# Where the copies behind a background sum of weight quarters are issued, and behind what, in a two-layer hybrid decoder trunk

## The chip, the core and the metric

The kernel runs on one core of a Trainium2 chip. The core has a matrix engine (PE in the profile; its weight loads are listed apart as PEld), a vector engine (DVE), a scalar engine (ACT), a general-purpose engine (POOL) and a sequencer that here only issues transfers (SP). Sixteen DMA engines move the data; SP, ACT and POOL each have a queue from which they issue transfers to them. Each engine works through its own instruction stream in order; semaphores tie the streams together.

The metric is the device time of one execution in microseconds (us), lower being better. Times shown are the median over several runs; a profile is one further execution with a trace.

## The reference

The program takes 512 tokens of width 1024 through two layers and a final norm. All arithmetic is float32.

```python
for l in range(DEPTH):                      # DEPTH = 2
    h = rms_norm(x, norm_mix[l])
    (m_qk, m_v, m_o, m_i, m_f, r_x, r_g, a_q, a_k, a_v, a_qi, a_ki, a_w, gates) = split(h @ w_in[l])
    ...                                     # mLSTM -> y_a;  RG-LRU -> y_b;  selected sparse attention -> y_c
    merged = (g_a * (y_a @ w_branch[l, 0]) + g_b * (y_b @ w_branch[l, 1])
              + g_c * (y_c @ w_branch[l, 2]))
    x = x + merged @ w_out[l]
    h = rms_norm(x, norm_ffn[l])
    ff_g, ff_u = split(h @ ffn_up[l], 2)    # hidden width 3072
    ff_g = causal_dwconv(ff_g, ffn_conv_w[l], ffn_conv_b[l])
    x = x + (gelu(ff_g) * ff_u) @ ffn_down[l]
return rms_norm(x, norm_final)
```

## The kernel before

**Weights and their splits.** All large weights lie in one tensor, `wts`, cut into units of 128 partitions by 1024 values (512 KB). SP loads the units one after the other into two `raw` buffers (`dma_to`, L185). A float32 product is made of three products in the fast type: each unit is split into a high part `wh` (ACT, L216) and a low part `wl` (DVE, L217), and PE multiplies `wl` by the input's high part, `wh` by its low part, and `wh` by its high part (L262, L268 and L306). A usual group of eight input blocks is 24 such matmuls. `unit()` asks for splits up to three or four units ahead of use.

**The order of work.** A scheduler turns the program into one instruction stream per engine. It simulates the program with its own idea of times, and sends each instruction as soon as that simulation finds the engine and the inputs free; instructions traced under `tc.high_priority()` go first among those ready. `tc.issue_after(i)`, here wrapped as `after(i)`, adds one rule: what is traced inside may not stand ahead of `i` on `i`'s own engine. On the chip the streams then run in just that order.

**A layer** begins with the norm of four tiles of 128 tokens (`Norm`: the sum of squares, its power -0.5 as `rs` on POOL, the scaled tile `xn` on DVE, transposes on PE, and a split into `xh`, `xl`). Then come the sections `mv` (four units), `sm` (one group; the gate rows, from which POOL writes `gd` to memory and later spreads it over all partitions as `g`), `rx` (four groups, each followed in the background by two matmuls of the RG-LRU gates), `qk` (eight groups), the rotary pairs `qi`, `q` and `k`, `av` and `mo`. In the first layer alone DVE and ACT also make the rotary tables (`rope_tables`). After the branches and `w_out` come a second norm and the feed-forward part in three chunks.

**The quads.** In ten places of each layer's feed-forward part (`QUADS`), two gate columns and two up columns are computed by a scheme that needs seven instead of eight half-size products (`quads`, L296). It needs four sums of weight quarters, which the kernel makes in device memory ahead of use: `b = w0 + w1`, `c = w1 + w2`, `e = w0 + c`, `g = w3 + e`. Each sum is a memory-to-memory copy of 512 KB, followed by a second transfer of 512 KB that adds into the copy. Twenty quads times four sums make 80 copies and 80 additions. The input side needs sums too: `x_sums` (L1030, L1033) adds and subtracts quarters of `xh + xl` on DVE.

**How the weight sums are issued before.** `g_sums` is a generator; `tick()` draws from it every third (then second, then fourth) slot of a counter that goes up by one with every half group or so. Each draw issues one transfer on POOL's queue (L144). Nothing but the data orders these transfers.

```python
def put(dst, src, **kw):
    G.dma_start(out=dst, in_=src, max_dma_last_dim=1024, **kw)
```

Below are the functions that the change touches.

Of the kernel before, what the change touches and what calls it, by code (L numbers as in the profile page):

```python
# [15 lines left out]
ALU = mybir.AluOpType  # L16
# [28 lines left out]
def tile_trunk(ctx, tc, x, pos, wts, chan, rgw, const, norm_mix, norm_ffn, norm_final, out, depth=2, dbg=None):  # L45
    nc = tc.nc
    V, A, T, G = nc.vector, nc.scalar, nc.tensor, nc.gpsimd

    def pool(name, bufs, **kw):
        return ctx.enter_context(tc.tile_pool(name=name, bufs=bufs, **kw))  # L50
# [4 lines left out]
    slot = pool("slot", 1)  # L55
# [21 lines left out]
    def S1(tag, shape=(P, 4, 512), dt=F32):  # L77
        return slot.tile(list(shape), dt, tag=tag, name=tag)
# [35 lines left out]
    for l in range(depth):  # L114
        u = l * per
        ffn = u + per - (NH // HC) * 3 * HC
        plan += [(u + i, None) for i in range(ffn - u)]
        u = ffn
# [10 lines left out]
    st = dict(dma=0, spl=0, use=0, slot=0)  # L129
    raws, spl, alt, own = {}, {}, {}, {}  # L130
    wsum = {}
# [8 lines left out]
            extra.add(i)  # L140

    def g_sums():
        def put(dst, src, **kw):
            G.dma_start(out=dst, in_=src, max_dma_last_dim=1024, **kw)  # L144

        def first_(u):
            w = wsum[u]
            for k, n in (("b", 0), ("c", 1), ("e", 0), ("g", 3)):
                yield put(w[k], wts[u + n])

        def then(u):
            w = wsum[u]
            for k, src in (("b", wts[u + 1]), ("c", wts[u + 2]), ("e", w["c"]), ("g", w["e"])):
                yield put(w[k], src, accum_op=ALU.add)

        gs = list(wsum)
        yield from first_(gs[0])
        for u, v in zip(gs, gs[1:] + [None]):
            f = first_(v) if v is not None else iter(())
            for _ in then(u):  # L160
                yield 1
                yield next(f, None)

    bg = g_sums()

    def held(l):
# [48 lines left out]
    def hl_split(ps, h, l):  # L215
        a = A.activation(out=h, in_=ps, func=AF.Copy)  # L216
        v = V.tensor_tensor(out=l, in0=ps, in1=h.bitcast(F32), op=ALU.subtract)  # L217
        return a, v

    def after(ins):  # L220
        return tc.issue_after(getattr(ins, "ins", ins))
# [2 lines left out]

    def tick():
        st["slot"] += 1
        p = st["slot"] % 308
        if p > 8 and p % (3 if p < 170 else 2 if p < 220 else 4) == 0:
            next(bg, None)

    def pump():
        tick()
        for g in list(streams):
            if g[1]:
                with tc.high_priority():
                    r = next(g[0], None)
            else:
                r = next(g[0], None)
            if r is None:
                streams.remove(g)  # L240
# [47 lines left out]
    def q_mm(ps, x, start=True):  # L288
        tick()
        h, l = [w.rearrange("p (k c) -> p k c", c=2 * P) for w in unit()]  # L290
        for j in (1, 0):
            i = 0
            for k in range(4):
                for a, b in ((l, 0), (h, 1), (h, 0)):
                    i += 1
                    T.matmul(ps[:, j * 256:(j + 1) * 256], lhsT=a[:, k, j * P:(j + 1) * P], rhs=x[b][:, k, :],  # L296
                             start=start and j == 1 and i == 1, stop=j == 0 and i == 12,
                             skip_group_check=True)
# [205 lines left out]
    for l in range(depth):  # L504
        if l == 0:
            res["src"] = x
            nrm = Norm(norm_mix[0:1, :], ("S1", "S2", "S4", "S5"))
# [7 lines left out]
            v = nrm.scaled(0)  # L515
# [7 lines left out]
            with after(st["pair"][0]), after(st["pair"][1]):  # L523
                v = nrm.scaled(1)
# [7 lines left out]
                with after(a1[1]):  # L532
                    v = nrm.scaled(2)
# [3 lines left out]
                    v = nrm.scaled(3)  # L537
# [8 lines left out]
        e = SimpleNamespace()  # L546
# [471 lines left out]
        nrm = Norm(norm_ffn[l:l + 1, :], ("S9", "S6"))  # L1018
# [7 lines left out]
        def x_sums():  # L1026
            qa, qb = [S1(g, (P, 2, 4, 256)) for g in ("S6", "S9")]
            a = [qa[:, 0], qa[:, 1], qb[:, 0], qb[:, 1]]
            for n in (2, 3, 0, 1):
                V.tensor_tensor(out=a[n], in0=xq[n][0].bitcast(F32), in1=xq[n][1].bitcast(F32), op=ALU.add)  # L1030
            for key, g, d, i0, i1, op in (("b", "S1", 3, 2, 3, ALU.subtract), ("c", "S2", 2, 0, 2, ALU.subtract),
                                          ("e", "S3", 0, 3, 0, ALU.subtract), ("f", "S7", 1, 1, 0, ALU.add)):
                V.tensor_tensor(out=a[d], in0=a[i0], in1=a[i1], op=op)  # L1033
                o = S1(g, (P, 2, 4, 256), dt=FR)
                hl_split(a[d], o[:, 0], o[:, 1])
                xq[key] = (o[:, 0], o[:, 1])
# [41 lines left out]
            for j in range(2):  # L1078
                hidden(i + j, m + j, gt[:, j, :], up[j])

        x_sums()
        nch = NH // HC
        for cidx in range(nch):
            hh = [S1("S4", dt=FR), S1("S6", dt=FR)]
# [2 lines left out]
            while i < HC:  # L1087
                m = cidx * HC + i
# [14 lines left out]
            if end:  # L1103
                nrm = Norm(norm_final[0:1, :] if last else norm_mix[l + 1:l + 2, :], ("S1", "S2"))
# [159 lines left out]
```

## Time and profile before

| | |
|---|---|
| time, median of three runs | 2179.81 us (2177.36 to 2180.73) |
| the profiled execution | 2172.2 us, of which the span of its instructions is 2170.4 us |
| PE busy | 1909.3 us, 88% of the span |
| DVE busy | 1265.5 us, 58% |
| ACT busy | 863.1 us, 40% |
| POOL busy | 223.1 us, 10% |
| moved by DMA | 333.74 MB, mean 154 GB/s |

In the views below a row of a timeline reads: start, duration (us), engine, line, operation, output<-inputs, and in brackets how long the engine idled before and what released it. A window's row gives, for a stretch of time, each engine's busy microseconds and number of instructions, the granted clock of PE, the mean share of the sixteen DMA engines that was busy, and the rate.

### The profile page before, as it was taken

To read this page: it belongs to the slowest core of one execution; us is meant where nothing else is said; L and a number is where in the kernel's file an instruction comes from. 1 tells how busy PE (TensorE), PEld (TensorE's weight loads), DVE (VectorE), ACT (ScalarE), POOL (GpSimd) and SP (SyncE) were. 2 spreads that over 40 slices of the span, in tenths; PEclk is the share of its full clock that TensorE was granted. 3 is DMA by queue.
4 is the path that set the end of the run, shared out by engine and by line. 5 is a ranking of instruction groups with operands and counts; after the bars stand their busy time and mean duration, and the time that the engine had idled before them with its cause. 6 is when DMAs were issued, how large, how long until landed. Compare 5 with 4: busy or idle time off the path is not lost.

```text
span 2170.4 us, 26601 instructions
## 1 busy us (share of the span) xinstructions
PE 1909.3 (88%) x10380; PEld 1627.7 (75%) x10380; DVE 1265.5 (58%) x2131; ACT 863.1 (40%) x1309; POOL 223.1 (10%) x314
## 2 busy tenths in 40 slices
PE   2366006999999999999999999999999999999998
PEld 1244004888888888989899878888888788999896
DVE  1252006786864447647667579777834457667584
ACT  1133004444444235425345466444342334445353
POOL 3433432121000000000000101210000000000000
PEclk6678557999999999999999999999999999999999
DMA  9999999675232332435454325853232233455452
GB/s 324 280 288 283 218 202 233 187 212 144 78 100 93 94 110 94 154 109 185 136 163 145 135 88 154 240 155 93 69 121 87 90 114 126 137 157 165 132 175 82
DMA packets 121758, 333.74 MB, mean 154 GB/s; under 512 B 10904, under 2 KB 52376, under 8 KB 119584
## 3 DMA queue, kind: packets, MB, share of 16 engines
q1 hardware_dynamic: 55584, 200.30, 29.2%
q0 software_dynamic: 64320, 127.44, 24.7%
q10 hardware_dynamic: 1728, 4.31, 0.6%
q8 instruction: 81, 1.33, 0.3%
q14 instruction: 45, 0.37, 0.1%
HBM read 312.06 MB, written 103.30 MB: 191 GB/s over the span
## 4 chain that ended last, share of the span: by engine, by line
PE 81%; DMA 14%; DVE 3%; issue 1%; ACT 1%; POOL 0%; POOLq 0%; ACTq 0%; DVEq 0%
PE A L262 25%; PE A L306 19%; PE A L268 12%; PE s L296 11%; PE t L296 5%; DMA wsc<-in_wts_dram 5%; DMA wsb<-in_wts_dram 5%; PE o L296 2%; DMA wse<-wsc 2%; PE o L836 1%; DMA wse<-in_wts_dram 1%; DMA wsg<-in_wts_dram 1%; PE o L762 1%; PE s L797 1%; PE t L849 1%
## 5 line engine op out<-in xcount | busy, mean ns | idle before, releaser
L262 PE MATMUL A<-xh,wl 128*128 128x512 f32 (+1 forms) x1072 | 428.5, 402 | 158.8 <-DVE wl L217 157.7
L217 DVE TENSOR_TENSOR wl<-raw,wh 128x1024 fp32r<-128x1024 f32 x294 | 358.8, 1222 | 350.2 <-ACT wh L216 348.1
L262 PE MATMUL A<-xl,wh 128*128 128x512 f32 (+1 forms) x1072 | 424.4, 398 | 4.2 <-DVE xl L217 4.2
L216 ACT ACTIVATE wh<-raw 128x1024 fp32r<-128x1024 f32 x294 | 309.8, 1056 | 296.7 <-PE A L306 127.5
L262 PEld LDWEIGHTS A<-xh,wl 128*128 128x128 f32 x1072 | 207.0, 193 | 213.7 <-DVE wl L217 154.8
L268 PE MATMUL A<-xh,wh 128*128 128x512 f32 (+1 forms) x1072 | 275.5, 391 | 0.0
L306 PE MATMUL A<-wh,S 128*128 128x512 f32 x832 | 256.1, 390 | 0.0
L262 PEld LDWEIGHTS A<-xl,wh 128*128 128x128 f32 x1072 | 207.2, 193 | 50.3 <-DVE xl L217 4.9
L268 PEld LDWEIGHTS A<-xh,wh 128*128 128x128 f32 x1072 | 195.5, 188 | 43.0 <-issue 0.5
L306 PEld LDWEIGHTS A<-wh,S 128*128 128x128 f32 x832 | 156.3, 188 | 33.3
L306 PE MATMUL A<-wl,S 128*128 128x512 f32 x416 | 162.6, 394 | 0.0
L296 PE MATMUL s<-S,wh 128*128 128x256 f32 x768 | 138.8, 282 | 0.0
L296 PEld LDWEIGHTS s<-S,wh 128*128 128x128 f32 x768 | 118.8, 190 | 0.2
L296 PE MATMUL s<-S,wl 128*128 128x256 f32 x384 | 108.1, 282 | 0.0
L469 DVE SCALAR_TENSOR_TENSOR m<-A,ch,m 128x511 f32<-128x511 f32 (+2 forms) x88 | 64.8, 744 | 46.1 <-ACT m L465 45.2
L306 PEld LDWEIGHTS A<-wl,S 128*128 128x128 f32 x416 | 78.1, 188 | 16.4
L399 POOL TENSOR_TENSOR rs<-rs,half 128x1 f32<-128x1 f32 x16 | 8.9, 557 | 743.8 <-DVE rs L398 730.7
L417 PE MATMUL s<-kst,xn 128*128 128x128 f32 x128 | 19.6, 301 | 72.1 <-DVE xn L383 72.1
L788 DVE TENSOR_TENSOR dmb<-g,kst 128x128 f32<-128x128 f32 x32 | 8.9, 285 | 116.1 <-DMA g<-gd 115.0
L262 PE MATMUL A<-S,wl 128*128 128x512 f32 x192 | 75.6, 395 | 0.5 <-ACT S L687 0.5
L262 PE MATMUL A<-S,wh 128*128 128x512 f32 x192 | 75.1, 393 | 0.0
L296 PEld LDWEIGHTS s<-S,wl 128*128 128x128 f32 x384 | 73.0, 190 | 0.2
(292 smaller groups left out, 3569.3 us busy)
## 6 DMA issues: line engine op xcount, KB each, us to landing
raw<-in_wts_dram SPq DMA_DIRECT2D x266, 512.0 KB, 3.6
wsb<-in_wts_dram POOLq DMA_DIRECT2D x40, 512.0 KB, 16.6
wsc<-in_wts_dram POOLq DMA_DIRECT2D x40, 512.0 KB, 16.9
quad<-in_wts_dram SPq DMA_DIRECT2D x28, 512.0 KB, 3.7
wse<-in_wts_dram POOLq DMA_DIRECT2D x20, 512.0 KB, 15.3
wsg<-in_wts_dram POOLq DMA_DIRECT2D x20, 512.0 KB, 15.7
wse<-wsc POOLq DMA_DIRECT2D x20, 512.0 KB, 18.3
wsg<-wse POOLq DMA_DIRECT2D x20, 512.0 KB, 21.5
```

The source lines that it names most:

```text
L216: a = A.activation(out=h, in_=ps, func=AF.Copy)
L217: v = V.tensor_tensor(out=l, in0=ps, in1=h.bitcast(F32), op=ALU.subtract)
L262: T.matmul(ps, lhsT=a[:, k, :], rhs=b[:, k, :], start=(i == 0), stop=False)
L268: T.matmul(ps, lhsT=wh[:, k, :], rhs=b_h[:, k, :], start=False, stop=(i == n))
L296: T.matmul(ps[:, j * 256:(j + 1) * 256], lhsT=a[:, k, j * P:(j + 1) * P], rhs=x[b][:, k, :], start=start and j == 1 and i == 1, stop=j == ...
L306: T.matmul(ps, lhsT=a[k0 + j][:, tt], rhs=b[:, j, :], start=(start and i == 1), stop=(stop and i == n))
L417: ins = T.transpose(ps[:, c * P:(c + 1) * P], xn[:, k * P:(k + 1) * P], ident)
L469: V.scalar_tensor_tensor(out=acc[:, d:], in0=ps[:, :S - d], scalar=ch[:, cw + j * step:cw + j * step + 1], in1=acc[:, d:], op0=ALU.mult, o ...
L762: T.matmul(po[:, 0:129], lhsT=SD[:, sb * P:(sb + 1) * P], rhs=e.mv[:, sb, h, :], start=(sb == 0), stop=(sb == tb))
L797: T.matmul(ps[:, sb * P:(sb + 1) * P], lhsT=e.qkF[1][:, h, sb * P:(sb + 1) * P], rhs=e.qkF[0][:, h, ts], start=True, stop=True)
L836: T.matmul(po[:, h * 64:(h + 1) * 64], lhsT=pc[:, c * P:(c + 1) * P], rhs=e.av[:, c, h * 64:(h + 1) * 64], start=(c == 0), stop=(c == t))
L849: T.transpose(pp[:, c * P:(c + 1) * P], pt[c // (t + 1)][:, c % (t + 1) * P:(c % (t + 1) + 1) * P], ident)
```

## The change

The 80 copies are issued from ACT's queue instead of POOL's. The 80 additions stay on POOL, each drawn one step after its copy. `tick()` now draws every sixth slot (past the first 14 of every 308), and a draw issues one copy and the previous copy's addition. Each draw stands under `after(st["pair"][0])`: `st["pair"][0]` is the ACT instruction of the latest weight unit's split, so the copy may not stand ahead of it in ACT's stream. The second part binds `x_sums` behind `nrm.last[1]`, the DVE instruction of the input's last split.

```diff
     def g_sums():
-        def put(dst, src, **kw):
-            G.dma_start(out=dst, in_=src, max_dma_last_dim=1024, **kw)
-
-        def first_(u):
-            w = wsum[u]
-            for k, n in (("b", 0), ("c", 1), ("e", 0), ("g", 3)):
-                yield put(w[k], wts[u + n])
-
-        def then(u):
-            w = wsum[u]
-            for k, src in (("b", wts[u + 1]), ("c", wts[u + 2]), ("e", w["c"]), ("g", w["e"])):
-                yield put(w[k], src, accum_op=ALU.add)
-
-        gs = list(wsum)
-        yield from first_(gs[0])
-        for u, v in zip(gs, gs[1:] + [None]):
-            f = first_(v) if v is not None else iter(())
-            for _ in then(u):
+        late = []
+        for u, w in wsum.items():
+            for k, n, m in (("b", 0, wts[u + 1]), ("c", 1, wts[u + 2]), ("e", 0, w["c"]), ("g", 3, w["e"])):
+                nc.scalar.dma_start(out=w[k], in_=wts[u + n], max_dma_last_dim=1024)
+                late.append((w[k], m))
+                if len(late) > 1:
+                    dst, src = late.pop(0)
+                    G.dma_start(out=dst, in_=src, max_dma_last_dim=1024, accum_op=ALU.add)
                 yield 1
-                yield next(f, None)
+        dst, src = late.pop(0)
+        G.dma_start(out=dst, in_=src, max_dma_last_dim=1024, accum_op=ALU.add)
+        yield 1
 
     def tick():
         st["slot"] += 1
-        p = st["slot"] % 308
-        if p > 8 and p % (3 if p < 170 else 2 if p < 220 else 4) == 0:
-            next(bg, None)
+        if st["slot"] % 308 > 14 and st["slot"] % 6 == 0:
+            with after(st["pair"][0]):
+                next(bg, None)
 
-        x_sums()
+        with after(nrm.last[1]):
+            x_sums()
```

A line of the old program is found eight lines higher in the new one (L216 is L208, L217 is L209), behind `x_sums` seven lines higher.

**POOL, first layer, from the rotary tables to the first spread of `gd`.** `ws...` are the sums in memory; `cs` holds the rotary tables, `gd` the gate rows, `g` their spread. Before:

```order
L460 DMA cs<-sinT 128x512
L460 DMA cs<-cosT 128x512
L144 DMA wse_178<-wsc_177 512x256
L144 DMA wsb_204<-in_wts_dram 512x256
L144 DMA wsc_205<-in_wts_dram 512x256
L614 DMA gd<-S_552 4x512
...
L574 DMA S_543<-cs 32x2x512 x2
L144 DMA wsg_179<-wse_178 512x256
L144 DMA wse_206<-wsc_205 512x256
L773 DMA g_1205<-gd 128x512
```

Between the write of `gd` and its first use 25 transfers of sums stand in POOL's stream, 23 of them in the rows left out, and 113 stand ahead of `cs`. Of the change, the same place:

```order
L368 TENSOR_TENSOR rs<-rs,half 128x1 x4
L452 DMA cs<-sinT 128x512
L452 DMA cs<-cosT 128x512
L566 DMA S_542<-cs 32x2x512 x2
L150 DMA wsb_152<-in_wts_dram 512x256
L606 DMA gd<-S_551 4x512
L765 DMA g_1202<-gd 128x512
```

The first addition of all now stands between the tables and `gd`; no transfer of a sum stands ahead of the tables or between `gd` and `g`.

**ACT, first layer, the `rx` groups.** `m` is the convolution's start from the group's result `A`, `S<-s` are the RG-LRU gates of the group before, `wh<-raw` is a weight unit's split. Before:

```order
L465 ACTIVATE m_639<-A,ch 128x512
L885 ACTIVATE S_603<-s,ch 128x512
L889 ACTIVATE S_604<-s,bx 128x512
L216 ACTIVATE wh<-raw 128x1024
L465 ACTIVATE m_682<-A,ch 128x512
```

These four steps come once per group: the split for the next group stands behind the gates of the last one. Of the change:

```order
L457 ACTIVATE m_637<-A,ch 128x512
L208 ACTIVATE wh<-raw 128x1024
L588 ACT_TABLE_LOAD
L588 ACTIVATE g_554<-g_554 4x512
L457 ACTIVATE m_680<-A,ch 128x512
L208 ACTIVATE wh<-raw 128x1024
L457 ACTIVATE m_723<-A,ch 128x512
L208 ACTIVATE wh<-raw 128x1024
L146 DMA wsb_152<-in_wts_dram 512x256
L877 ACTIVATE S_602<-s,ch 128x512
```

Three splits now stand ahead of the first gate, and the first copy of a sum stands right behind the third of them.

**DVE, first layer, the start of the feed-forward part.** `xl<-s,xh` are splits of the input, `S<-xh,xl` the first additions of `x_sums`. Before:

```order
L217 TENSOR_TENSOR xl<-s,xh 128x4x128
L401 SCALAR_TENSOR_TENSOR xn<-S_4218,rs,grow 128x512
L1030 TENSOR_TENSOR S_5022<-xh,xl 128x1024 x2
L217 TENSOR_TENSOR xl<-s,xh 128x4x128 x2
L217 TENSOR_TENSOR wx<-quad,wx 128x1024
```

Of the change:

```order
L209 TENSOR_TENSOR xl<-s,xh 128x4x128
L393 SCALAR_TENSOR_TENSOR xn<-S_4214,rs,grow 128x512
L209 TENSOR_TENSOR xl<-s,xh 128x4x128 x2
L1022 TENSOR_TENSOR S_5018<-xh,xl 128x1024 x2
L1022 TENSOR_TENSOR S_5019<-xh,xl 128x1024 x2
```

The last two splits of the input have moved ahead of the first two additions.

## The prediction

> **What bounds the kernel now.** I read the page's slices first, to see where PE idles, since PE is busy for 88% of the span.
>
> ```profile
> PE   2366006999999999999999999999999999999998
> PEclk6678557999999999999999999999999999999999
> DMA  9999999675232332435454325853232233455452
> ```
>
> Each digit is one fortieth of the span, 54 us. PE is full from the eighth slice on. In the first seven it is idle most of the time, PE's granted clock is low, and the DMA engines are full. So the time to be had lies in the first 400 us, and the rest can only be lost. Next I cut that front into stretches, and set beside them a stretch of the second layer in which PE does the same sections (first `sm` group to the first rotary step) and one of the feed-forward part.
>
> ```profile
> 29.90:120.60 90.70, 34.01 (x124) 25.80 (x124) 17.59 (x44) 14.79 (x28) 34.41 (x47) 0.66 1.09 291
> 120.60:210.00 89.40, 55.93 (x165) 36.72 (x166) 39.50 (x60) 27.18 (x31) 34.74 (x44) 0.77 1.12 283
> 210.00:342.00 132.00, 3.22 (x14) 2.25 (x12) 17.17 (x28) 18.61 (x26) 54.23 (x57) 0.53 1.21 212
> 342.00:398.76 56.76, 52.32 (x221) 42.26 (x222) 35.94 (x55) 21.08 (x34) 8.47 (x11) 0.92 0.94 218
> 860.00:1240.00 380.00, 379.79 (x2476) 346.40 (x2475) 247.12 (x325) 175.54 (x225) 5.69 (x10) 1.00 0.46 147
> 1247.40:1338.42 91.02, 91.02 (x393) 70.47 (x392) 77.70 (x113) 60.08 (x83) 4.52 (x9) 1.00 0.35 107
> ```
>
> The stretches are cut at these rows of the timeline: the first matmul behind `mv` and the first rotary product of each layer.
>
> ```profile
> 120.62 0.50 PE L262 MATMUL A<-xh,wl 128*128 128x512 f32 x1 [2.89 <-DVE wl L217]
> 398.76 0.69 DVE L493 TENSOR_TENSOR m<-A,cosT 128x512 f32<-128x512 f32 x1
> 1247.40 0.40 PE L262 MATMUL A<-xh,wl 128*128 128x512 f32 x1
> 1338.42 0.68 DVE L493 TENSOR_TENSOR m<-A,cosT 128x512 f32<-128x512 f32 x1
> ```
>
> From 120.60 to 398.76 the first layer runs 165 + 14 + 221 = 400 matmuls in 278.16 us; the second runs 393 in 91.02 us with PE never idle. Then I asked who waits for whom, and what POOL does meanwhile.
>
> ```profile
> DVE xn L383 <- POOL rs L376: 74.8, 3, 29.2
> DVE dmb L788 <- DMA g<-gd: 115.0, 2, 112.3
> 240.21 0.55 POOL L614 DMA_DIRECT2D gd<-S  x1 [1.91 <-DMA wse<-wsc]
> 307.71 0.61 POOL L773 DMA_DIRECT2D g<-gd  x1 [1.44 <-DMA wsc<-in_wts_dram]
> 356.52 1.01 POOL L144 DMA_DIRECT2D wsg<-wse  x1 [1.58 <-DMA wsg<-wse]
> 359.17 1.01 POOL L144 DMA_DIRECT2D wsg<-wse  x1 [1.64 <-DMA wsg<-wse]
> ```
>
> All 160 transfers of the sums stand early in POOL's stream, and each waits for an older one: one every 2.65 us (359.17 - 356.52). The small things behind them wait too: three powers of the first norm (74.8 us of DVE's time), and `g`, issued 67 us after `gd` and keeping DVE idle for 112.3 us. The chain of waits says the same: it runs from 4.55 us to 323.75 us almost wholly through such transfers.
>
> ```profile
> 4.55 17.42 DMA wsc<-in_wts_dram
> ...
> 286.46 20.97 DMA wsc<-in_wts_dram
> 307.71 16.03 DMA g<-gd
> ```
>
> The stretch 120.60 to 210.00 has a second cause, the order itself. ACT's rows show one group:
>
> ```profile
> 166.27 0.78 ACT L465 ACTIVATE m<-A,ch 128x512 f32<-128x512 f32 x1 [8.76 <-PE A L268]
> 171.52 0.69 ACT L885 ACTIVATE S<-s,ch 128x512 f32<-128x512 f32 x1 [4.48 <-PE s L884]
> 173.23 0.69 ACT L889 ACTIVATE S<-s,bx 128x512 f32<-128x512 f32 x1 [1.02 <-PE s L888]
> 173.82 1.05 ACT L216 ACTIVATE wh<-raw 128x1024 fp32r<-128x1024 f32 x1
> ...
> 191.08 1.05 ACT L216 ACTIVATE wh<-raw 128x1024 fp32r<-128x1024 f32 x1
> ```
>
> No bracket on the split: it waits for no load, it stands behind the gates. Each group is split, multiplied and drained before the next split begins: 17.3 us from split to split, where PE in the second layer needs 24 x 91.02 / 393 = 5.6 us per group.
>
> **The change part by part.** (1) *The front.* In the new POOL stream nothing stands ahead of the first powers, and only one addition between the rotary tables and `gd`. The three waits of DVE shrink to the power itself, 0.56 us each by its row here:
>
> ```profile
> 61.53 1.11 POOL L376 TENSOR_TENSOR rs<-rs,half 128x1 f32<-128x1 f32 x2
> ```
>
> That is 74.8 - 3 x 0.56 = 73 us. PE idles through these waits, so I count them whole. (2) *`sm` to the first rotary product.* Both the wait for `g` and the late splits go, since three splits now stand ahead of the first gate. I take the second layer's time for the same work: 278.2 - 91.0 = 187 us less. The first layer has the rotary tables to make besides, two rounds of this kind and six steps of under half a microsecond:
>
> ```profile
> 121.93 2.87 DVE L451 SCALAR_TENSOR_TENSOR th<-g,th 128x512 f32<-128x512 f32 x4
> 125.80 2.87 DVE L451 SCALAR_TENSOR_TENSOR th<-g,th 128x512 f32<-128x512 f32 x4
> ```
>
> some 9 us of DVE, which has 91.02 - 77.70 = 13 us free in that stretch. They fit, but not always when they are due: 0 to 9, I take +5. (3) *`x_sums`.* Its first two additions stand ahead of the input's last splits, and PE waits for these, in both layers:
>
> ```profile
> 844.89 2.36 DVE L1030 TENSOR_TENSOR S<-xh,xl 128x1024 f32<-128x1024 f32 x2 [2.95 <-PE s L417]
> 847.17 1.28 DVE L217 TENSOR_TENSOR xl<-s,xh 128x512 fp32r<-128x512 f32 x2
> 1788.53 0.39 PE L262 MATMUL A<-xl,wh 128*128 128x256 f32 x1 [2.12 <-DVE xl L217]
> 891.90 5.75 PE s L296 x48
> ```
>
> Bound behind the splits, the additions cost PE nothing there: -2.1 us twice, -4. What is late next are their own results, wanted only at the first quad (the last row, the first of the chain to multiply them), 47 us after the first addition; eight additions and four splits of some 1.2 us each fit in. Bounds 0 and -4.
>
> (4) *The copies on ACT.* ACT issued transfers in this trace too, and so does SP:
>
> ```profile
> 64.83 0.33 ACTq L928 DMA_DIRECT2D S<-in_rgw_dram  x1
> 65.31 0.59 ACT L216 ACTIVATE xh<-s 128x512 fp32r<-128x512 f32 x1
> 2.12 1.13 SPq L185 DMA_DIRECT2D raw<-in_wts_dram  x1
> ```
>
> The transfer that stands between two splits of the input is issued in 0.33 us while the first still runs, and the second starts on time. A copy of a sum has four times as many rows as those transfers, and no row here prices it: 0.33 us from below, 1.13 us (the longest seen at issue) from above. Each stands behind a unit's split, of 1.05 us by the row above, which covers it; ACT is 40% busy besides. I take 0; without cover 80 x 1.13 = 90 us of ACT, of which splits made three units ahead would keep most off PE, say 20 at worst.
>
> (5) *The traffic, now under a full PE.* The same bytes move, spread over some 1500 us (from the first layer's `rx` to the second's first quad). How PE fares beside saturated transfers can be read at 342.00 to 398.76: 0.94 of the DMA engines, PE idle 56.76 - 52.32 = 4.4 us, 8%. The 160 transfers at 2.65 us are 424 us at that density: 33 us if every one costs this, 0 if the units loaded ahead cover all. In most places a transfer has neighbours only for a moment, so I take a third, +12.
>
> (6) *POOL's waits.* An addition waits for its copy to land, and what stands behind it in POOL's stream waits too: `dh`, `dl` of the rotary pairs, and the powers of the second norm, where the new stream has an addition between the second and third. Landing times:
>
> ```profile
> raw<-in_wts_dram SPq DMA_DIRECT2D x266, 512.0 KB, 3.6
> wsb<-in_wts_dram POOLq DMA_DIRECT2D x40, 512.0 KB, 16.6
> ```
>
> A copy that meets little else should be nearer to the 3.6 us of a unit's load than to 16.6 us, which is the time with eight in the queue. At a norm the addition then holds the power for perhaps 2 us; four norms' worth of such places, and the rotary steps: 0 to 20, I take +4.
>
> *The sum*, against the profiled span: 2170.4 - 73 - 187 + 5 - 4 + 0 + 12 + 4 = 1927.4 us. The median shown is 2179.81, 9.4 us above that span, so the forecast is **1937 us**.
>
> **The rivals.** *The traffic hurts where PE is fed most tightly.* In a quad two units' 48 matmuls take 5.75 us by the chain's row, so one unit 2.9, and a load 3.6 us. If a copy and its addition together hold the loads up for 2 x 2.65 = 5.3 us at each of some 20 steps in the first layer's feed-forward part, that adds 106 us: about 2040. For it: four buffers are all that is loaded ahead there. Against it: the DMA share there is 0.46, and 5.3 us is about two units, which the buffers hold.
>
> In the Trainium skill, "DMA: Bandwidth & Descriptors", section "Issuing engines are not separate DMA queues" speaks against the change: transfers from the scalar, sync and gpsimd engines run on the same 16 DMA engines and interleave, and issuing from several only saves the sequencer's time. By that rule alone moving the copies would gain nothing. *The move is only a move*, then, is a rival: the transfers crowd the front as before, from another queue, and the time stays at 2180. The trace bears the sharing out (both kinds land late while the engines are full), but the order speaks against the rest: the first copy stands behind the split of a fourth `rx` unit, and the others are strung along the units.
>
> *The front keeps its order-bound part.* If the `rx` groups still ran one by one at the 17.3 us that ACT's splits show instead of 5.6, four groups cost 4 x 11.7 = 47 us: 1984. The new order has the splits ahead, so this needs the loads to be late.
>
> *Slower: POOL becomes a gate everywhere.* If a copy lands only after 16.6 us also when spread, every urgent POOL instruction behind an addition (about 35 places in both layers: powers, `g`, `dh` and `dl` groups, `hr`) waits some 11 us beyond a unit's 5.6, on PE's path since PE's order is fixed: 35 x 11 = 385, less the 243 us gained: about 2320. It decides from 243 / 35 = 7 us per place. For it: only that no trace shows a lone copy. Against: the load's 3.6 us.
>
> **How the numbers follow.** The forecast's case, with all costs between their bounds, has 70%; a little below it, if the profile's distance to the median shrinks, 3%; the quads 11%; the order-bound front 8%; POOL as a gate 5%; the mere move 2%; 1% is left for a slower case unnamed. All costs at nothing give 2170.4 - 73 - 187 - 4 = 1906, with 9.4 added 1916; all at their upper bounds (9, 0, 20, 33, 20) 1992, with 9.4 added 2002. The range 1908 to 1995 holds the forecast's case nearly whole and the order-bound front. Three runs spread by 0.15%, so 0.2% is about what can be told from no change. Faster 0.92, same 0.02, slower 0.06.
>
> **What would show it.** Right: PE's slices full from about the second on; the first rotary product near 145 us instead of 398.76; no `xn` wait of over 1 us for `rs` in the first norm; no wait of PE for `xl` at the feed-forward start; copies landing in 3 to 7 us; PE idle less than 30 us in all behind 145 us. Wrong: PE waiting for `wl` behind `raw` loads in the quads (traffic), for `wl` in the `rx` groups (order), or DVE for `rs` and `g` behind additions (POOL). The forecast falls if these come to more than 60 us together, or if ACT's splits wait behind an issue that takes longer than a split.

## The result and the profile after

The changed kernel takes 1913.62 us in the median of four runs (1913.00 to 1914.99); the kernel before, beside it, 2178.59 us. The ratio is 0.8785, with a 95% interval of 0.877 to 0.8801: 12% faster. The forecast was 1937 us with a range of 1908 to 1995. Sign and range hold; the forecast is 23 us too high, and the terms of that miss are named below.

The page's slices of the changed kernel (one digit is a fortieth of the span, 48 us):

```profile
span 1911.2 us, 26675 instructions
PE   8999999999999999999999999999999999999998
PEclk9999999999999999999999999999999999999999
DMA  5468975556568768778645798655556576353542
```

PE is full from the second slice on, its granted clock is high from the start, and the transfer engines, which were full for the first seven slices, are now busy at a middling rate to the end. They move the same 333.7 MB. Next the windows view, cut at the same landmarks as before: first matmul of `mv`, first matmul of `sm`, first rotary product, first matmul of the feed-forward part, and the last three again for the second layer. The columns are the stretch and its length, the busy time of PE, PEld, DVE, ACT and POOL, PE's granted clock, the share of the transfer engines, and GB/s.

```profile
0.00:10.57 10.57, 8.51 (x29) 3.35 (x29) 4.08 (x11) 3.87 (x6) 0.76 (x5) 1.00 0.82 293
10.57:41.29 30.72, 27.56 (x124) 20.81 (x125) 21.63 (x51) 15.39 (x28) 2.15 (x3) 1.00 0.44 143
41.29:133.26 91.97, 91.27 (x392) 70.52 (x391) 81.38 (x120) 61.58 (x80) 11.35 (x16) 1.00 0.55 155
133.26:584.83 451.57, 447.17 (x2214) 371.99 (x2212) 279.83 (x592) 180.55 (x333) 55.98 (x78) 1.00 0.66 175
584.83:983.28 398.45, 398.32 (x2577) 362.38 (x2577) 265.43 (x342) 187.10 (x238) 29.24 (x33) 1.00 0.74 205
983.28:1074.13 90.85, 90.85 (x392) 70.29 (x391) 76.96 (x112) 59.59 (x80) 8.88 (x13) 1.00 0.57 151
1074.13:1530.97 456.84, 447.93 (x2214) 371.92 (x2212) 279.00 (x591) 179.53 (x329) 55.97 (x78) 1.00 0.65 173
1530.97:1911.20 380.23, 372.40 (x2448) 340.92 (x2448) 252.05 (x319) 172.31 (x217) 7.34 (x9) 1.00 0.49 154
```

The old kernel's trace has the first `mv` matmul at 29.91 us and the feed-forward parts at 845.05 and 1785.67 us; the other cuts are shown with the prediction. Two of its rows, from the rotary product to the feed-forward part in each layer, are needed below:

```profile
398.76:845.05 446.29, 445.56 (x2205) 370.96 (x2203) 276.63 (x580) 178.73 (x325) 33.03 (x55) 1.00 0.41 124
1338.42:1785.67 447.25, 445.84 (x2212) 371.08 (x2211) 279.91 (x591) 180.01 (x329) 33.56 (x56) 1.00 0.42 124
```

So the 259.2 us between the two spans (2170.4 - 1911.2) lie here:

| stretch | before | after | difference | the prediction's term |
|---|---|---|---|---|
| start to first `sm` matmul | 120.62 | 41.29 | -79.33 | (1) -73 |
| first `sm` matmul to first rotary product | 278.14 | 91.97 | -186.17 | (2) -187 + 5 |
| rotary product to feed-forward part, layer 1 | 446.29 | 451.57 | +5.28 | (5), (6) |
| feed-forward part, layer 1 | 402.35 | 398.45 | -3.90 | (3) -2 |
| `sm` to rotary product, layer 2 | 91.02 | 90.85 | -0.17 | (5), (6) |
| rotary product to feed-forward part, layer 2 | 447.25 | 456.84 | +9.59 | (5), (6): +16 in all |
| feed-forward part, layer 2, to the end | 384.73 | 380.23 | -4.50 | (3) -2 |

How the front got short can be read from POOL's timeline and from DVE's waits in the first 60 us:

```profile
7.28 0.55 POOL L368 TENSOR_TENSOR rs<-rs,half 128x1 f32<-128x1 f32 x1 [6.83 <-DVE rs L367]
69.38 1.14 POOL L150 DMA_DIRECT2D wsb<-in_wts_dram  x1 [11.74 <-DMA wsb<-in_wts_dram]
79.00 0.56 POOL L606 DMA_DIRECT2D gd<-S  x1 [8.48 <-DVE S L604]
81.98 1.15 POOL L765 DMA_DIRECT2D g<-gd  x2 [2.43 <-DMA gd<-S]
DVE xn L375 <- POOL rs L368: 1.4, 2, 0.7
```

The first power stands ahead of every transfer, `g` follows `gd` by 3 us instead of 67, and DVE's 74.8 us of waiting for powers are 1.4 us. The first rotary product comes at 133.26 us, where the prediction looked for it near 145.

PE's waits in the whole trace, the largest groups (total us, times, longest):

```profile
PE s L695 <- DMA dl<-m: 3.2, 1, 3.2
PE A L298 <- DVE wl L209: 2.7, 4, 1.1
PE s L695 <- DMA S<-dl: 2.3, 1, 2.3
PE s L409 <- ACT xn L392: 2.2, 1, 2.2
PE t L676 <- DVE S L811: 2.2, 2, 1.8
PE s L695 <- ACT g L698: 1.9, 1, 1.9
```

No wait for `xl` at the feed-forward part, none for `wl` there: the four for `wl` in the second row stand in the first `mv`, before 36 us. What is left stands at the rotary pairs (`dl`, `S`, `g`, L695), at the second norm (`xn`, L409) and just behind the rotary pairs (L676). The copies' issues and landings, by the rows of line 146 (duration in ns: minimum, median, maximum; first and last start) and of the transfers (KB, us to landing):

```profile
L146 ACTq DMA_DIRECT2D wsb<-in_wts_dram x20: 497/497/638, 64.0 to 1537.9; - x20
wsb<-in_wts_dram ACTq DMA_DIRECT2D x20, 512.0 KB, 5.0
wsb<-in_wts_dram POOLq DMA_DIRECT2D x20, 512.0 KB, 7.3
```

An issue costs ACT 0.50 us; a copy of `wsb` lands in 5.0 us and an addition to it in 7.3 us (16.6 before, both together). Behind the first rotary product PE is idle for 4.4 + 0.1 + 0 + 8.9 + 7.8 = 21 us by the windows, less than the 30 that the prediction allowed.

### The profile page after: what moved, and what is told of

It reads as the page before. It is cut to its first block, busy times and chain, and to the rows that moved or that the text cites. A ratio compares the mean times of both kernels' runs of the same rounds, so it can differ in the third digit from the quotient of the medians.

```text
span 1911.2 us, 26675 instructions
## 1 busy us (share of the span) xinstructions
PE 1884.0 (99%) x10380; PEld 1612.2 (84%) x10380; DVE 1260.4 (66%) x2131; ACT 859.9 (45%) x1308; POOL 171.7 (9%) x234
## 4 chain that ended last, share of the span: by engine, by line
PE 84%; DMA 7%; DVE 6%; ACT 2%; issue 1%; POOL 0%; ACTq 0%; POOLq 0%; DVEq 0%
PE A L254 24%; PE A L298 20%; PE A L260 12%; PE s L288 12%; PE t L288 6%; PE o L288 3%; DMA raw<-in_wts_dram 2%; PE o L828 2%; DVE wl L209 2%; DMA wsc<-in_wts_dram 1%; DMA wse<-in_wts_dram 1%; PE t L841 1%; DVE m L461 1%; DMA dl<-m 1%; PE s L789 1%
## 5 line engine op out<-in xcount | busy, mean ns | idle before, releaser
L209 DVE TENSOR_TENSOR wl<-raw,wh 128x1024 fp32r<-128x1024 f32 x294 | 358.9, 1222 | 328.3 <-ACT wh L208 325.3
L208 ACT ACTIVATE wh<-raw 128x1024 fp32r<-128x1024 f32 x294 | 310.1, 1056 | 281.9 <-PE A L298 113.8
L254 PE MATMUL A<-xh,wl 128*128 128x512 f32 (+1 forms) x1072 | 420.1, 394 | 2.2 <-DVE m L461 0.7
L254 PE MATMUL A<-xl,wh 128*128 128x512 f32 (+1 forms) x1072 | 417.5, 392 | 0.0
L260 PE MATMUL A<-xh,wh 128*128 128x512 f32 (+1 forms) x1072 | 279.8, 394 | 0.0
L254 PEld LDWEIGHTS A<-xh,wl 128*128 128x128 f32 x1072 | 201.5, 188 | 49.6 <-DVE wl L209 3.5
L254 PEld LDWEIGHTS A<-xl,wh 128*128 128x128 f32 x1072 | 201.9, 188 | 44.8 <-issue 2.2
L934 ACT ACTIVATE th<-A 128x512 f32<-128x512 f32 x48 | 28.6, 596 | 104.0 <-PE A L260 76.3
L843 ACT ACTIVATE g<-t 128x512 f32<-128x512 f32 (+2 forms) x48 | 25.2, 524 | 105.1 <-PE t L841 102.6
L298 PE MATMUL A<-wx,S 128*128 128x512 f32 x288 | 68.9, 393 | 0.0
```

Source lines behind the costliest of these rows:

```text
L254: T.matmul(ps, lhsT=a[:, k, :], rhs=b[:, k, :], start=(i == 0), stop=False)
L260: T.matmul(ps, lhsT=wh[:, k, :], rhs=b_h[:, k, :], start=False, stop=(i == n))
L298: T.matmul(ps, lhsT=a[k0 + j][:, tt], rhs=b[:, j, :], start=(start and i == 1), stop=(stop and i == n))
L843: A.activation(out=pT[:, :n * P], in_=pp[:, :n * P], func=AF.Copy)
L934: A.activation(out=th, in_=pg, func=AF.Tanh, scale=0.5)
```

## The experiments

Each run stands beside runs of the kernel before on the same chip; ratios are to those.

**1. The input sums alone, put in and taken out.** First the old kernel with this edit only:

```diff
-        x_sums()
+        with after(nrm.last[1]):
+            x_sums()
```

> The old kernel with one edit: its input sums are bound behind the input's last splits; copies and additions stay on POOL as they were. Theory: only the wait of PE for xl goes, 2.1 us in each layer; in the first layer PE's matmuls ran at half clock for 3.5 us behind that wait in the old trace, worth 1.9 us more, so 4.2 + 1.9 = 6.1 us less: about 2172.5 us against 2178.6. If the clock's dip has another cause: 2174.4. Rival: the wait only moves to the first quad, whose sums come later, and the time stays within 2 us of 2178.6.

Measured: 2169.19 us against 2175.01, ratio 0.9969 (0.9957 to 0.9982), so 4 to 9 us less; the medians differ by 5.8. PE's wait of 4.2 us for `xl` is gone from its list. Then the changed kernel with the edit reversed:

> The changed kernel with one edit: the input sums are free again, as in the old kernel; copies stay on ACT, bound. Theory: PE waits 2.1 us for xl in each layer again, 1913.6 + 4.2 = 1917.8 us, up to 1919.7 with a clock dip of 1.9 us behind one of the waits. Rival (the binding did nothing here): within 1.5 us of 1913.6. The rest of the gain, some 255 us, must stay in both cases.

Measured: 1916.59 us, ratio 0.8807 (0.879 to 0.8823). PE's list has the wait again:

```profile
PE A L254 <- DVE xl L209: 4.2, 2, 2.1
```

The time moves the expected way by about 3 us, but the interval overlaps with that of the changed kernel, so here only the trace tells. The first run shows that the binding pays; both say that nearly the whole gain, some 255 us, has nothing to do with it. The clock's dip, which the first run was to show as well, is not told apart by its time: the interval holds 4.2 and 6.1 us. The traces do tell it apart. The first layer's feed-forward part takes 402.35 us in the old kernel and 402.39 us in this second run, where the input sums are free, and 398.35 us in the first run and 398.45 us in the changed kernel, where they are bound. Of these 4 us the wait itself is 2.1; the rest goes with the slow clock behind it (granted 0.52 in the old kernel, see the last section).

**2. No sums at all, in both kernels.** Neither kernel issues a copy or an addition, and the quads load plain weight quarters:

```diff
-    bg = g_sums()
+    bg = iter(())
...
-            src = wts[u] if op is None else wsum[u][op] if op in wsum[u] else wts[u + {"a": 0, "d": 3, "f": 2}[op]]
+            src = wts[u] if op is None else wts[u + {"a": 0, "b": 1, "c": 2, "d": 3, "e": 1, "f": 2, "g": 3}[op]]
```

> The changed kernel without any copy or addition: the quads load plain weight quarters where they loaded sums, so 160 transfers and their results are left out; PE does the same matmuls. This prices ACT's issues, the traffic and POOL's waits together. Theory: the stretches from the rotary steps to the feed-forward part lose the 5.3 + 0.4 + 9.6 = 15 us which the changed kernel spends there beyond the old one: about 1898 us. Rival 1 (all of it is hidden under the matmuls, the extra time there is chance): 1912 to 1915. Rival 2 (the traffic costs PE in the feed-forward part too): below 1890.

> The old kernel without any copy or addition: the quads load plain weight quarters, 160 transfers and their results are left out. Theory: the whole front stall comes from them (POOL's queue, full transfer engines, and an order that was laid out around them), so the time falls to that of the changed kernel without sums plus 4 to 6 us for the free input sums: about 1903 us. Rival (the rx groups that run one by one at 17.3 us are the order's own doing): four groups at 11.7 us more each, about 1950 us.

Measured: the changed kernel without sums 1905.65 us (ratio 0.8757, 0.8743 to 0.8771), the old one without sums 1912.53 us (0.8791, 0.8777 to 0.8806). I had expected 1898 and 1903.

The second settles where the old front stall came from. Without sums the old kernel's first rotary product comes at 134.71 us, and its stretch from `sm` to there is 93.51 us:

```profile
41.20:134.71 93.51, 91.38 (x385) 70.34 (x384) 81.24 (x120) 61.44 (x80) 6.82 (x12) 0.98 0.36 113
```

So the `rx` groups ran one by one only beside the sums: without them ACT's splits stand ahead of the gates in the old kernel too. The rival at 1950 falls. The two kernels without sums differ by 6.9 us, with 4.2 us of waits for `xl` in the old one and PE's granted clock near half (0.53 and 0.50) for 3.5 us behind both of them.

The first needs its windows (from the rotary product to the feed-forward part in both layers, then the rest):

```profile
133.65:580.20 446.55, 445.37 (x2214) 371.03 (x2212) 280.15 (x592) 180.87 (x333) 33.58 (x56) 1.00 0.42 124
1069.50:1516.32 446.82, 445.64 (x2212) 371.13 (x2210) 279.76 (x591) 179.92 (x329) 33.58 (x56) 1.00 0.42 124
1516.32:1902.30 385.98, 372.36 (x2448) 340.88 (x2448) 252.06 (x319) 172.25 (x217) 2.20 (x4) 0.99 0.45 138
```

The two middle stretches lose 5.0 and 10.0 us against 451.57 and 456.84: the expected 15 us, which is thus the price of the sums in the changed kernel. In a second trace of the changed kernel (the repeat of experiment 5) the two take 447.77 and 459.36 us, 13.8 us more than without sums: the sum of the two holds, its split between the layers does not. But the last stretch is 5.8 us longer (380.23 before), with the same PE time to a twentieth of a microsecond. It lies behind the last instruction: the last store is issued some 10 us ahead of the span's end here, some 4 us in the changed kernel; in the old kernel without sums it is again 10 us. No row shows what that time is; it stays open, and it is why the span moved by 9 us and not by 15.

**3. Copies without additions.** The copies stay on ACT, the additions are left out, and the quads load plain quarters as above:

```diff
                nc.scalar.dma_start(out=w[k], in_=wts[u + n], max_dma_last_dim=1024)
-                late.append((w[k], m))
-                if len(late) > 1:
-                    dst, src = late.pop(0)
-                    G.dma_start(out=dst, in_=src, max_dma_last_dim=1024, accum_op=ALU.add)
                 yield 1
```

> The changed kernel with the 80 copies on ACT as they are and no addition; the quads load plain weight quarters, so the sums' results are left out. It parts the cost of the sums (8 us between the changed kernel and the one without sums). Theory (the additions carry it: they are what POOL waits with, and their packets fill most of the transfer engines' time): within 2 us of the kernel without sums, about 1906. Rival (ACT's issues of 0.50 us and the copies' traffic carry it): 1911 to 1914.

Measured: 1905.51 us, ratio 0.8748 (0.8726 to 0.8769), no different from no sums at all; the two middle stretches are 446.78 and 447.00 us. So 80 issues on ACT and 42 MB of copies, with no additions beside them, cost PE nothing that can be seen, and the 15 us belong to the additions: their traffic, and what stands behind them on POOL. This run does not part these two.

**4. Queue or binding?** The change moves the copies and binds them at the same time. Four runs take the two apart. All keep the changed kernel's pace and its input sums.

Copies on POOL, bound behind nothing that holds them (a binding behind an instruction of ACT does not hold POOL):

```diff
-                nc.scalar.dma_start(out=w[k], in_=wts[u + n], max_dma_last_dim=1024)
+                G.dma_start(out=w[k], in_=wts[u + n], max_dma_last_dim=1024)
```

> The changed kernel with its copies issued from POOL instead of ACT; pace and input sums as in the changed kernel. A copy on POOL can't be held behind ACT's split: in the order, 16 copies stand ahead of the first norm's power again and all 160 transfers early in POOL's stream, as in the old kernel. Theory (the place in the queues decides): the old kernel less the 6 us of the input sums, about 2171 us. Rival (the slower pace in the source is what helps): below 2100.

Copies on ACT, free:

```diff
-            with after(st["pair"][0]):
-                next(bg, None)
+            next(bg, None)
```

> The changed kernel with its copies on ACT, bound behind nothing: some 45 of them stand among ACT's first 60 instructions, and the additions that follow them stand early on POOL, 28 of them ahead of gd. Theory (the binding is what counts, not ACT): the front fills with transfers again; gd and g go behind about 28 additions and 80 copies, 108 x 2.65 = 286 us, so the first rotary product comes near 300 us instead of 133: about 2080 us, between 2030 and 2170. Rival (a queue of its own is enough): under 1950.

Copies on POOL, bound (`newest[0]` is the instruction that POOL was given last; the lines that keep it are left out):

```diff
-                nc.scalar.dma_start(out=w[k], in_=wts[u + n], max_dma_last_dim=1024)
+                G.dma_start(out=w[k], in_=wts[u + n], max_dma_last_dim=1024)
...
-            with after(st["pair"][0]):
+            with after(newest[0]):
```

> Copies and additions both on POOL, each step bound behind the newest instruction that POOL has been given, at the changed kernel's pace; ACT issues nothing of it. Theory (any engine does, if the steps are strung along the units): within 15 us of the changed kernel, 1906 to 1928, the copies' own issues of half a microsecond to 1.1 us standing in the way of the rotary transfers. Rival (a copy on POOL stands behind an addition that waits, so the front or the rotary steps stall): over 1950.

Copies on SP, bound behind the newest load of a unit:

```diff
-                nc.scalar.dma_start(out=w[k], in_=wts[u + n], max_dma_last_dim=1024)
+                nc.sync.dma_start(out=w[k], in_=wts[u + n], max_dma_last_dim=1024)
...
-            nc.sync.dma_start(out=r[1], in_=src)
+            st["load"] = nc.sync.dma_start(out=r[1], in_=src)
...
-            with after(st["pair"][0]):
+            with after(st["load"]):
```

> The copies on SP, each bound behind the newest load of a weight unit; additions on POOL, pace and input sums as in the changed kernel. Theory (any engine does): 1908 to 1920 us. Rival (a copy stands between two loads on SP, and the loads of units come later): PE waits for wl in the feed-forward part, 80 x 0.5 us to 80 x 1.1 us at most, 1925 to 2000.

| copies on | bound | us (median) | ratio to before | 95% interval |
|---|---|---|---|---|
| POOL | no | 2170.58 | 0.9962 | 0.9946 to 0.9978 |
| ACT | no | 2187.66 | 1.0048 | 1.0028 to 1.0069 |
| POOL | yes | 1925.76 | 0.8847 | 0.8827 to 0.8867 |
| SP | yes | 1921.80 | 0.8822 | 0.8782 to 0.8863 |
| ACT (the change) | yes | 1913.62 | 0.8785 | 0.877 to 0.8801 |

The binding makes nearly the whole gain, and the queue alone makes none. Unbound on POOL the kernel is the old one less the input sums, as expected, so the slower pace by itself is not what helps either. Bound on POOL it has 251 of the 265 us; ACT's queue adds about 12 us to that. In the traces POOL loses in the two stretches from `sm` to the rotary product (96.76 and 100.06 us, 91.97 and 90.85 with ACT) and in the first feed-forward part (404.62 and 398.45), 20.2 us in all, and wins 5.9 us back in the second layer behind the rotary product (450.99 and 456.84). What makes these 12 us stays open. For SP, whose runs spread from 1910.8 to 1928.0 us, the difference to ACT is not told apart from none.

Unbound on ACT I had missed: 2080 expected, and it is slower than the old kernel. Its slices, five rows of ACT's timeline and the row of all `wsb` issues show why:

```profile
PE   3310435999999999999999999999999999999997
PEclk7655666999999999999999999999999999999999
DMA  9999999885223233445544334862232333455452
123.99 4.22 ACTq L146 DMA_DIRECT2D wse<-in_wts_dram  x1
...
136.78 4.22 ACTq L146 DMA_DIRECT2D wsc<-in_wts_dram  x1
141.05 0.64 ACTq L146 DMA_DIRECT2D wse<-in_wts_dram  x1
141.73 7.22 ACTq L146 DMA_DIRECT2D wsg<-in_wts_dram  x1
148.99 1.06 ACT L208 ACTIVATE wh<-raw 128x1024 fp32r<-128x1024 f32 x1 [36.67 <-DMA wsc<-in_wts_dram]
L146 ACTq DMA_DIRECT2D wsb<-in_wts_dram x20: 497/1733/9761, 1.7 to 205.2; - x20
```

With one copy behind the other an issue is no longer 0.50 us. It takes 1.7 us in the median and up to 9.8 us, and holds ACT all that time. All 80 are issued by 211 us and take 187.8 us of ACT together (40.3 us in the changed kernel). The split that PE needs stands behind nine of them for 36.7 us. My sum for this run had the transfers' time and not ACT's.

Full transfer engines alone do not make an issue long. In the old kernel, with the engines as full (1.09), ACT issued `S<-in_rgw` in 0.33 us (shown with the prediction). Here the same transfer takes 2.30 us, while SP's loads take 0.33 us in the median and 0.84 us at most in the whole run:

```profile
43.62 2.30 ACTq L919 DMA_DIRECT2D S<-in_rgw_dram  x1
L177 SPq DMA_DIRECT2D raw<-in_wts_dram x266: 327/328/843, 1.2 to 2147.0; - x133
```

So the long issues go with the copies that pile up on ACT's own queue; which limit they meet there these runs don't show. The Trainium skill says in "DMA: Bandwidth & Descriptors", section "Issuing engines are not separate DMA queues", that issuing from several engines saves only the sequencer's time for the issue, "which is usually small relative to the DMA itself". This run agrees with the first half, since moving the copies alone gained nothing (1.0048). The second half holds here in the median (1.7 us beside landings of 12 us) but not at the longest (9.8 us).

**5. Another pace.** What is left of PE's waits stands where the rotary pairs are turned, and their small transfers land late there: `dl` in 8.2 us where the kernel without sums has 3.8 us. So the sums pause in those slots and run a little faster elsewhere; a second version also pauses behind them and at the second norm, and runs faster still:

```diff
-        if st["slot"] % 308 > 14 and st["slot"] % 6 == 0:
+        p = st["slot"] % 308
+        if p > 14 and not 34 <= p <= 62 and st["slot"] % 5 == 0:
```

and in the second version

```diff
-        if st["slot"] % 308 > 14 and st["slot"] % 6 == 0:
+        p = st["slot"] % 308
+        if p > 14 and not 34 <= p <= 84 and not 140 <= p <= 176 and st["slot"] % 4 == 0:
```

> The changed kernel itself, as the partner on the same chip for the three kernels that follow: 1911 to 1916 us.

> The changed kernel with another pace: no step of the sums in slots 34 to 62 of a layer, where the rotary pairs are turned, and one step in 5 slots elsewhere instead of one in 6. Theory (what is left of the stalls is the rotary transfers dh, dl and S meeting the sums' traffic and standing behind additions on POOL): PE's waits for them, 3.2 + 2.3 + 1.9 us, go, and about 2 us of half clock behind the first of them: 7 to 9 us under the changed kernel, about 1905. Rival (any denser stretch costs as much as the pause wins): the same time, within 2 us.

> As before this one, but the pause is slots 34 to 84 and 140 to 176 (rotary pairs, the step behind them and the second norm), one step in 4 slots elsewhere. Theory: the waits at the second norm (2.2 us) and behind POOL's power rp (1.8 and 0.5 us) go as well: 11 to 13 us under the changed kernel, about 1902. Rival: at one step in 4 slots the sums or the loads of units come late in the feed-forward part, and the time is that of the changed kernel or more.

Measured: the changed kernel again 1913.50 us (1907.5 to 1919.4, five runs), the first pause 1905.97 us (1905.5 to 1906.6, five runs; ratio 0.8751, 0.8729 to 0.8772), the second 1910.23 us (0.8774, 0.8751 to 0.8797). The first has the 7.5 us that were expected, and its runs don't overlap with those of its partner (0.9 us lie between them); it is the fastest kernel here that computes the whole. Its landing row and its middle stretches:

```profile
dl<-m POOLq DMA_DIRECT2D x24, 256.0 KB, 3.8
137.28:583.40 446.12, 445.36 (x2212) 370.48 (x2210) 279.69 (x592) 181.22 (x333) 55.50 (x78) 1.00 0.67 175
1075.83:1524.28 448.45, 444.63 (x2199) 369.25 (x2197) 279.35 (x591) 179.69 (x329) 54.45 (x77) 1.00 0.67 173
```

The two middle stretches gain 13.8 us; 6.8 us of that are lost again from `sm` to the rotary product (95.63 and 93.99 us, 91.97 and 90.85 in the changed kernel).

The second version has both middle stretches as short as without sums (446.48 and 446.22 us), but loses elsewhere: 97.89 us from `sm` to the rotary product in the second layer where the first version takes 93.99, with 4.2 us of PE's waits for `g` (L790) and `wl` in it. That stretch lies in the denser slots, so the denser pace probably costs there what the longer pause wins; pause and pace were not varied apart.

## Why the prediction was right, and where its numbers were off

*What bounds the kernel.* Right: the front was the place, and the sums were its only cause. Without them the old kernel has no front stall (experiment 2).

*(1) The front, -73.* It was 79.3. The waits went as reckoned. What I left out is the clock: while PE waited its matmuls ran slowly, and the `mv` stretch's PE time fell from 34.01 to 27.56 us as the granted clock rose from 0.66 to 1.00. These 6.5 us make up the miss.

*(2) `sm` to the rotary product, -187 + 5.* It was -186.2. The second layer's 91.0 us was the right measure, and the tables fit: 91.97 us in the first layer. The +5 was about 1.

*(3) The input sums, -4.* The waits of 2.1 us in each layer went. The two feed-forward stretches lost 8.4 us. In the first layer the old trace ran at half clock behind the wait, 1.7 us more (see below); the prediction left this out. In the second, about 2 us lie behind the last matmul (9.6 us to the end before, 7.7 after), in the tail that stayed open.

*(4) ACT's issues, 0.* Right for this kernel: 0.50 us each, between the bounds, under the units' splits, and experiment 3 finds no cost. My upper bound of 1.13 us was the wrong kind of bound, though. It holds because the copies are strung out, not because of the row it came from: with copies piled up on ACT's queue an issue takes up to 9.8 us (experiment 4).

*(5) and (6) Traffic and POOL, +12 and +4.* Together +14.7 by the table, 15 by experiment 2. The total was right by luck. I had read the 4.4 us of idle PE in the stretch from 342.00 to 398.76 as the price of full transfer engines, but they are one wait:

```profile
356.56 1.05 ACT L216 ACTIVATE wh<-raw 128x1024 fp32r<-128x1024 f32 x1
360.19 0.50 PE L262 MATMUL A<-xh,wl 128*128 128x512 f32 x1 [4.35 <-DVE wl L217]
```

The split has no bracket, so it waited for no load; it stood behind the group's `m`, as in the `rx` groups. The 8% and the 33 us worked out from it thus price the order and not the traffic, and the third that I took of them was a guess. Nor were the term's split and place right: I spread it over all transfers under a full PE, while the feed-forward part of the first layer, with the engines at 0.74, lost nothing, and it sits at the rotary pairs and the norm, where small transfers meet the additions. The copies have no part in it.

*The 9.4 us from span to median.* The weakest step. Time and span of one execution differ by 1.8 us in the profiled runs (2172.2 and 2170.4; 1913.0 and 1911.2). The rest was chance: over all experiments the old kernel's runs scatter from 2172 to 2187 us, and its profile was one of its fastest. The changed kernel scatters hardly less (1907.5 to 1919.4 us in experiment 5); in its first four runs its median lies 2.4 us above the profile. That is 7.0 of the miss. With such scatter the prediction's 0.2% from three runs was also too fine.

The misses add up: 6.3 + 4.2 + 4.4 + 1.3 + 7.0 = 23.2 us of the 23.4. All five have the same sign. That (5) and (6) fit best is no credit to their working.

*The rivals.* The quads kept their pace (no wait for `wl` there), and the `rx` groups did not stay order-bound. POOL did not become a gate: a spread copy lands in 5.0 us, not 16.6. The mere move is real, but only without the binding, and then it costs 0.5%.

## What to carry to other kernels

Background transfers cost by where they stand in the streams of the engines that issue them, not by their bytes: 80 copies strung along the weight units were free, and the same 80 at the head of ACT's or POOL's stream, with their additions behind them, cost some 255 to 275 us. Bind each to an instruction that the main work has to reach anyway, keep them away from the places where small transfers are on the path, and try the binding apart from the move. A profile is one execution: before an offset between its time and the median is added to a forecast, look whether it is fixed or scatter.

## What the runs showed of the hardware beside that

A short wait of PE can cost twice. Windows of the changed kernel behind its five largest single waits (3.18, 2.32, 1.87, 1.75 and 2.24 us), then of the old kernel behind the 2.12 us wait for `xl`, first and second layer; the last three columns are granted clock, share of the transfer engines and GB/s:

```profile
163.18:167.50 4.32, 4.32 (x17) 3.85 (x18) 1.23 (x5) 1.63 (x6) 0.44 (x1) 0.60 0.59 241
1101.53:1106.00 4.47, 4.47 (x14) 3.56 (x15) 0.65 (x2) 0.38 (x1) 0.00 (x0) 0.62 1.04 396
1170.64:1175.00 4.36, 4.36 (x20) 3.69 (x21) 4.29 (x16) 1.92 (x6) 1.06 (x2) 1.00 0.65 176
1210.72:1215.00 4.28, 4.28 (x21) 3.61 (x22) 3.04 (x11) 2.29 (x4) 0.92 (x1) 1.00 1.05 189
1510.20:1514.50 4.30, 4.30 (x23) 3.71 (x24) 3.36 (x7) 3.19 (x8) 0.56 (x1) 1.00 0.72 113
848.84:852.37 3.53, 3.53 (x15) 3.18 (x14) 3.50 (x4) 0.00 (x0) 0.00 (x0) 0.52 0.39 128
1789.50:1793.00 3.50, 3.50 (x25) 3.18 (x24) 3.47 (x4) 0.00 (x0) 0.00 (x0) 1.00 0.44 137
```

Behind three of these seven waits the granted clock is near half for 3 to 4 us (3.53 us at 0.52 costs 3.53 x 0.48 = 1.7 us), behind the other four it is full; the same wait of 2.12 us does it in one layer and not in the other, and in both layers of the old kernel without sums. The Trainium skill's "TensorE: Matmul & The Clock Gate", section "What's actually happening", ties half clock to an idle window of about 3.4 us that runs freely and does not start anew with a kernel; the length of the slow stretch agrees, but waits of 2.1 to 3.2 us, shorter than that, were enough here. Which of them trigger it, these runs don't show.

The second thing is the issue that holds its engine: a copy's issue takes 0.50 us with the copies strung out, and 1.7 us in the median and 9.8 us at most with them piled up on ACT's queue, while SP's loads beside the same full transfer engines are issued in 0.84 us or less (experiment 4).
